# Half loads of the plain block behind runs of seven-product steps, and the second step of the next pair loaded behind the border's plain blocks

## The chip, the cores and the metric

The kernel runs on one core of one Trainium2 chip. The metric is the device time of one execution in microseconds, the median over several runs; lower is better. Matmuls run on TensorE (PE in the profile, its weight loads PEld), element work on VectorE (DVE), ScalarE (ACT) and GpSimd (POOL); SyncE (SP) issues most of the loads.

## What is computed

The reference is one layer of a decoder trunk on 256 tokens (16 meta tokens ahead of them): retention and mLSTM heads with one input and one output projection, and then a gated MLP with a short causal convolution. Only the last part matters here:

```python
up = causal_dwconv(u @ w_up, ffn_conv_w, ffn_conv_b)
gate, val = jnp.split(up, [FFN_DIM], axis=-1)        # FFN_DIM = 5632
h = h + (jax.nn.silu(gate) * val) @ w_down           # (256, 5632) @ (5632, 2048)
return rmsnorm(h, norm_final)[:, N_META:]
```

All is float32.

## The kernel before

**Three products for one.** Every float32 operand is split into a high part (a cast, on ACT) and a low part (operand less high part, on DVE), and a product is made of three matmuls: high by high, low by high, high by low. So for a weight block of 128 x 1024 (`wraw`) ACT writes `whi`, DVE writes `wlo`, and PE takes the block's matmuls with `whi` first and those with `wlo` behind them. `wraw` tiles come from a ring of four, `whi` and `wlo` from rings of five each (`load_w`, L113 to L122). A load into `wraw` waits until the tile that stood in its slot has been read for the last time, by DVE as a rule.

**The down projection.** The FFN is worked on in two halves (L744): 22 tiles of the up projection, and then the down projection over these 22 tiles in 11 *steps* `q` of two tiles (256 rows of `w_down`) each. The 2048 output columns are four blocks `b` of 512, taken in two *pairs* (0, 1) and (2, 3); the 256 tokens are two halves `tt`. Within a pair the steps follow each other in the order of `steps` (L924): 0 to 10, and in the last pair of the second half 0, 1, 4, 2, 7, 3, 5, 6, 8, 9, 10. There are two kinds of steps:

- A *plain* step (`PLAIN`, steps 0, 4, 9, 10; 7 and 8 too in the last pair) loads one block of 512 KB for each `j` of the pair's two column blocks (`load_step`, L909, through L116) and does 12 matmuls of 512 columns with it (`product`, L814, matmuls in L828).
- A *seven-product* step (`FAST`, steps 1, 2, 3, 5, 6, 7, 8) multiplies the 2 x 2 blocks of tokens, rows and columns with seven products in place of eight (`seven`, L830). It loads a sum that was formed early and kept in DRAM (`kept`, 256 KB, L838) and three weight blocks (768 KB, L839) into one of two buffers, `left[turn]`, which take turns (their name in the profile is `hT`, whose memory they use). DVE forms two differences, `ta` (128 x 1024, L842) and the first half of `tb` (128 x 512, L843), in two tiles of the `wraw` ring; the second half of `tb` stays empty. Four casts (L764) and four subtractions (L766) follow, and 21 matmuls (L857, L858, L860).

So steps 1, 2, 3 and 5, 6, 7, 8 stand in runs between the plain steps 0, 4, 9 and 10. At the end of a pair its sums leave PSUM (`share`, L878, and L949) and are added to the result by DMAs of POOL (L876), while the next pair's step 0 begins. That place is called the *border* here.

**What sets the order.** The tile framework orders each engine's instructions by a model of their times; engines then run their rows in order, each waiting for what it needs. `tc.issue_after(x)` forbids an instruction to stand ahead of `x`. A load on SP that must wait for a slot holds up all loads behind it.

Of the kernel before, what the change touches and what calls it, by code (L numbers as in the profile page):

```python
# [11 lines left out]
F32R = mybir.dt.float32r  # L12
# [71 lines left out]
def trunk(ctx: ExitStack, tc: tile.TileContext, io, out: bass.AP):  # L84
# [659 lines left out]
    for half in range(2):  # L744
# [18 lines left out]
        def split(hi, lo, x, after=None):  # L763
            copied = nc.scalar.copy(hi, x)  # L764
            with tc.issue_after(after.ins) if after else nullcontext():
                return copied, nc.vector.tensor_tensor(out=lo, in0=x, in1=hi.bitcast(F32), op=ALU.subtract)  # L766
# [60 lines left out]
            for n, (a, m, i) in list(enumerate(parts))[n0:n1]:  # L827
                nc.tensor.matmul(ps, a, m[:, i, cols], start=first and n == 0, stop=seed or last and n == 5, skip_group_check=seeded)  # L828

        def seven(b, q, cs, ps, first, last, after, norm):  # L830


            nonlocal turn
# [1 line left out]
            raw = left[turn]  # L835
            turn = 1 - turn

            nc.sync.dma_start(raw[:, 0, :], early[b, q])  # L838
            nc.sync.dma_start(raw[:, 1:4, :], io["wd7"][b // 2, half * NQD + q][:, 1:4, :])  # L839
            ta, tb = (wpool.tile([P, 2, 512], F32, name="wraw", bufs=4) for _ in range(2))  # L840

            nc.vector.tensor_tensor(out=ta, in0=raw[:, 0:1, :].to_broadcast([P, 2, 512]), in1=raw[:, 1:3, :], op=ALU.subtract)  # L842
            nc.vector.tensor_tensor(out=tb[:, 0, :], in0=raw[:, 3, :], in1=raw[:, 0, :], op=ALU.subtract)  # L843
# [65 lines left out]
        def load_step(b, q, to=wpool):  # L909
            return load_w(io["wd"][b, half * NQD + q], [P, 2, 512], to)  # L910
# [4 lines left out]
        for b in (0, 2):  # L915
            cs = {}
            for j in range(2):
                for tt in range(2):
                    cs[tt, j] = at.tile([P, 512], F32, name="atps")
            ps = [mm.tile([P, 512], F32, name="mmps") for _ in range(4)]  # L920

            final = half == 1 and b == 2
            steps = [0, 1, 4, 2, 7, 3, 5, 6, 8, 9, 10] if final else range(NQD)
            fast = [q for q in steps if q in FAST and not (final and q in BOTH)]  # L924
            plain = [q for q in steps if q not in fast]
            alone = plain[-lag:] if final else []
            for q in steps:
                if q in fast:
                    due = []
                    if final and q != fast[0]:  # L930
                        due, gains = gains[:1], gains[1:]
                    seven(b, q, cs, ps, q == fast[0], q == fast[-1], emptied, due)
                    if q == fast[-1]:
                        with tc.high_priority() if final else nullcontext():
                            share(ps, b, final)
                    continue
                for j in range(2):
                    if j == 1 and q in alone:
                        continue
                    w = load_step(b + j, q)  # L940
                    for tt in range(2):
                        product(cs[tt, j], tt, q, w, q == plain[0], q == plain[-1 - (lag if final and (tt, j) == (1, 1) else 0)])
            for j in range(2):
                for n, tt in enumerate(range(2)):
                    c = (b + j) * 512
                    if not final:

                        x = x_tile((4, 3, 1, 0)[2 * j + n])
                        emptied = nc.scalar.copy(x, cs[tt, j])  # L949
                        onto(tt, b + j, x)  # L950
                        if half == 1:
                            gains.append((tt, b + j, c, c + 512))
                    elif j == 0:
                        add(cs[tt, j], tt, c)
                        squares(tt, b, c, c + 512)
                        times_gain(tt, c, c + 512)
# [116 lines left out]
```

## Time and profile before

| | us |
|---|---|
| median of three runs | 1205.56 (1204.94 to 1208.27) |
| the profiled execution | 1206.01 |
| its span on the core | 1204.2 |
| down projection, first half of the FFN | 717.5 to 829.2 of the span |
| down projection, second half | 1083.3 to 1196.6 |

The profile is of one execution. Its rows give start and length in us from the start of the span; the time of the whole execution is 1.81 us more than the span. A matmul's row is longer than its share of PE's time, since matmuls overlap: their rate is read from the distance of their starts. Where a row of a timeline ends in brackets, the engine stood idle before it for so long, and the bracket names what ended that.

### The profile page before, as it was taken

The numbers are of one execution on the slowest core, as the hardware profiler recorded it, in microseconds if no ns is written. First come the engines' busy times: TensorE is split into PE (matmuls) and PEld (weight loads), VectorE is DVE, ScalarE is ACT, GpSimd is POOL, SyncE is SP. The second block draws the span as 40 slices with busy tenths as digits, with TensorE's granted clock in tenths as the row PEclk, the third lists the DMA queues.
The fourth block names the chain that finished last, engine by engine and source line by source line (L and its number), as shares of the span: only waits on it lengthen the run. The fifth ranks groups of instructions, "written<-read, shape, count | busy, mean of one in ns | idle before, by whom it ended". The sixth has DMA issues, their size and how long they took to land.

```text
span 1204.2 us, 22798 instructions
## 1 busy us (share of the span) xinstructions
PE 1194.5 (99%) x8956; PEld 1151.2 (96%) x8956; DVE 971.1 (81%) x1446; ACT 708.1 (59%) x964; POOL 167.3 (14%) x222
## 2 busy tenths in 40 slices
PE   9999999999999999999999999999999999999997
PEld 9999999999999999999999998878999999998886
DVE  8967778766775966788888889997697878789897
ACT  8747746655656656555555556665554655556664
POOL 0100001111110311021112100202023112100232
PEclk9999999999999999999999999999999999999999
DMA  8865565566565965766866744949777767755956
GB/s 280 275 208 162 169 187 169 197 182 192 171 189 168 345 204 176 252 219 203 263 217 212 225 178 175 272 182 272 279 249 250 234 247 242 253 184 211 281 170 200
DMA packets 83005, 263.27 MB, mean 219 GB/s; under 512 B 14673, under 2 KB 18897, under 8 KB 82769
## 3 DMA queue, kind: packets, MB, share of 16 engines
q1 hardware_dynamic: 71952, 223.85, 56.9%
q0 software_dynamic: 10368, 37.11, 10.1%
q8 instruction: 70, 1.15, 0.4%
q10 hardware_dynamic: 576, 0.85, 0.2%
q14 instruction: 39, 0.31, 0.1%
HBM read 243.42 MB, written 11.27 MB: 211 GB/s over the span
## 4 chain that ended last, share of the span: by engine, by line
PE 97%; DMA 1%; DVE 1%; ACT 0%; issue 0%; SPq 0%; DVEq 0%; ACTq 0%
PE mmps L128 26%; PE mmps L129 25%; PE mmps L131 25%; PE atps L828 8%; PE mmps L860 2%; PE mmps L857 2%; PE mmps L858 2%; PE atps L858 1%; PE atps L857 1%; PE atps L860 1%; PE atps L380 1%; DMA wraw<-in_wd 1%; PE atps L372 0%; DMA hT<-in_xT 0%; PE atps L128 0%; PE atps L131 0%
## 5 line engine op out<-in xcount | busy, mean ns | idle before, releaser
L119 ACT CAST whi<-wraw 128x1024 fp32r<-128x1024 f32 x352 | 368.5, 1049 | 311.0 <-PE mmps L129 200.9
L121 DVE TENSOR_TENSOR wlo<-wraw,whi 128x1024 fp32r<-128x1024 f32 x352 | 432.5, 1231 | 68.9 <-ACT whi L119 66.7
L128 PE MATMUL mmps<-uh,whi 128*128 128x258 f32 x1408 | 346.1, 283 | 0.0
L129 PE MATMUL mmps<-ul,whi 128*128 128x258 f32 x1408 | 346.0, 283 | 0.0
L128 PEld LDWEIGHTS mmps<-uh,whi 128*128 128x128 f32 x1408 | 267.6, 190 | 0.1
L129 PEld LDWEIGHTS mmps<-ul,whi 128*128 128x128 f32 x1408 | 267.1, 190 | 0.1
L128 PE MATMUL mmps<-xh,whi 128*128 128x272 f32 (+2 forms) x864 | 219.8, 288 | 0.0
L129 PE MATMUL mmps<-xl,whi 128*128 128x272 f32 (+2 forms) x864 | 218.3, 286 | 0.0
L131 PE MATMUL mmps<-uh,wlo 128*128 128x258 f32 x1408 | 196.5, 282 | 0.0
L131 PEld LDWEIGHTS mmps<-uh,wlo 128*128 128x128 f32 x1408 | 179.9, 189 | 0.0
L129 PEld LDWEIGHTS mmps<-xl,whi 128*128 128x128 f32 x864 | 162.9, 189 | 0.0
L128 PEld LDWEIGHTS mmps<-xh,whi 128*128 128x128 f32 x864 | 162.5, 188 | 0.1
L131 PE MATMUL mmps<-xh,wlo 128*128 128x272 f32 (+2 forms) x864 | 126.6, 285 | 0.0
L131 PEld LDWEIGHTS mmps<-xh,wlo 128*128 128x128 f32 x864 | 114.2, 188 | 0.0
L764 ACT CAST whi<-hT 128x1024 fp32r<-128x1024 f32 x52 | 53.6, 1052 | 26.5 <-PE atps L828 7.9
L681 DVE TENSOR_TENSOR cu<-mmps,rstd 128x258 f32<-128x258 f32 x88 | 37.3, 424 | 38.1 <-PE mmps L131 37.5
L766 DVE TENSOR_TENSOR wlo<-hT,whi 128x1024 fp32r<-128x1024 f32 x52 | 62.2, 1221 | 5.9 <-ACT whi L764 4.7
L129 PE MATMUL mmps<-mixl,whi 128*128 128x258 f32 x256 | 63.0, 283 | 0.0
L128 PE MATMUL mmps<-mixh,whi 128*128 128x258 f32 x256 | 62.4, 282 | 0.0
L766 DVE TENSOR_TENSOR wlo<-wraw,whi 128x1024 fp32r<-128x1024 f32 (+1 forms) x52 | 52.2, 1038 | 0.9 <-PE mmps L860 0.2
L764 ACT CAST whi<-wraw 128x1024 fp32r<-128x1024 f32 (+1 forms) x52 | 43.0, 837 | 16.5 <-PE mmps L858 7.1
L876 POOL DMA_DIRECT2D hn<-x x27 | 23.6, 1033 | 202.6 <-ACT x L882 174.8
(284 smaller groups left out, 1732.9 us busy)
## 6 DMA issues: line engine op xcount, KB each, us to landing
wraw<-in_wu SPq DMA_DIRECT2D x176, 512.0 KB, 4.5
wraw<-in_wi SPq DMA_DIRECT2D x108, 512.0 KB, 4.1
hT<-in_wd SPq DMA_DIRECT2D x26, 768.0 KB, 4.6
wraw<-in_wd SPq DMA_DIRECT2D x36, 512.0 KB, 4.9
wraw<-in_wo SPq DMA_DIRECT2D x32, 512.0 KB, 4.1
x<-in_wd POOLq DMA_DIRECT2D x13, 768.0 KB, 7.5
hn<-x POOLq DMA_DIRECT2D x27, 256.0 KB, 7.9
hT<-kept SPq DMA_DIRECT2D x26, 256.0 KB, 2.8
```

The costliest lines, as they stand in the source:

```text
L119: nc.scalar.copy(hi, raw)
L121: nc.vector.tensor_tensor(out=lo, in0=raw, in1=hi.bitcast(F32), op=ALU.subtract)
L128: nc.tensor.matmul(ps, hi[:, k, :], xh(kk), start=kk == first, stop=False)
L129: nc.tensor.matmul(ps, hi[:, k, :], xl(kk), start=False, stop=False)
L131: nc.tensor.matmul(ps, lo[:, k, :], xh(kk), start=False, stop=kk == last)
L681: evacuated = nc.vector.tensor_tensor(out=u, in0=ps[:, :NQ], in1=rstd2, op=ALU.mult)
L764: copied = nc.scalar.copy(hi, x)
L766: return copied, nc.vector.tensor_tensor(out=lo, in0=x, in1=hi.bitcast(F32), op=ALU.subtract)
L828: nc.tensor.matmul(ps, a, m[:, i, cols], start=first and n == 0, stop=seed or last and n == 5, skip_group_check=seeded)
L857: nc.tensor.matmul(o, sh[:, f, m, :], hi[:, i, :], start=begin, stop=False)
L858: nc.tensor.matmul(o, sl[:, f, m, :], hi[:, i, :], start=False, stop=False)
L860: nc.tensor.matmul(o, sh[:, f, m, :], lo[:, i, :], start=False, stop=end)
```

## The change

There are two edits, both in the down projection.

**Half loads.** Where a run of at least two seven-product steps is followed by a plain step, the first block of this plain step (`j` = 0) is no longer loaded into a tile of its own. The second halves of `tb` of the run's last two steps are collected in `spare`, and in the run's last step, behind its own load (`asked`), two loads of 256 KB each fill them. The plain step then casts and subtracts the two halves one after the other (`split`, L764 and L766) into one `whi` and one `wlo`. This happens seven times: at steps 4 and 9 of each pair but the last, and at step 8 of the last pair. The bytes loaded and the matmuls stay the same.

**The held step.** In the second pair of each half (`b == 2`) the load of the second seven-product step may not be issued ahead of the last block load that stands ahead of it in the program (`last_load`, set in `load_w`): that of step 0, `j` = 1, in the first half, and of step 4, `j` = 1, in the second.

```diff
@@ -827,7 +827,7 @@
             for n, (a, m, i) in list(enumerate(parts))[n0:n1]:
                 nc.tensor.matmul(ps, a, m[:, i, cols], start=first and n == 0, stop=seed or last and n == 5, skip_group_check=seeded)
 
-        def seven(b, q, cs, ps, first, last, after, norm):
+        def seven(b, q, cs, ps, first, last, after, norm, held, pieces):
 
 
             nonlocal turn
@@ -835,9 +835,18 @@
             raw = left[turn]
             turn = 1 - turn
 
-            nc.sync.dma_start(raw[:, 0, :], early[b, q])
-            nc.sync.dma_start(raw[:, 1:4, :], io["wd7"][b // 2, half * NQD + q][:, 1:4, :])
+            with tc.issue_after(last_load.ins) if held else nullcontext():
+                nc.sync.dma_start(raw[:, 0, :], early[b, q])
+                asked = nc.sync.dma_start(raw[:, 1:4, :], io["wd7"][b // 2, half * NQD + q][:, 1:4, :])
             ta, tb = (wpool.tile([P, 2, 512], F32, name="wraw", bufs=4) for _ in range(2))
+            for n, i in pieces:
+                if i == 0:
+                    spare.append(tb[:, 1, :])
+                else:
+                    spare.append(tb[:, 1, :])
+                    for i, x in enumerate(spare):
+                        with tc.issue_after(asked.ins):
+                            nc.sync.dma_start(x, io["wd"][b, half * NQD + n][:, i, :])
 
             nc.vector.tensor_tensor(out=ta, in0=raw[:, 0:1, :].to_broadcast([P, 2, 512]), in1=raw[:, 1:3, :], op=ALU.subtract)
             nc.vector.tensor_tensor(out=tb[:, 0, :], in0=raw[:, 3, :], in1=raw[:, 0, :], op=ALU.subtract)
@@ -924,12 +933,15 @@
             fast = [q for q in steps if q in FAST and not (final and q in BOTH)]
             plain = [q for q in steps if q not in fast]
             alone = plain[-lag:] if final else []
-            for q in steps:
+            spare = []
+            for n, q in enumerate(steps):
                 if q in fast:
                     due = []
                     if final and q != fast[0]:
                         due, gains = gains[:1], gains[1:]
-                    seven(b, q, cs, ps, q == fast[0], q == fast[-1], emptied, due)
+                    pieces = [(steps[n + 2 - i], i) for i in range(2)
+                              if steps[n + 2 - i] in plain and all(m in fast for m in steps[n - i : n + 2 - i])]
+                    seven(b, q, cs, ps, q == fast[0], q == fast[-1], emptied, due, b == 2 and q == fast[1], pieces)
                     if q == fast[-1]:
                         with tc.high_priority() if final else nullcontext():
                             share(ps, b, final)
@@ -937,7 +949,13 @@
                 for j in range(2):
                     if j == 1 and q in alone:
                         continue
-                    w = load_step(b + j, q)
+                    if j == 0 and spare:
+                        w = [wpool.tile([P, 2, 512], F32R, name=name, bufs=5) for name in ("whi", "wlo")]
+                        for i, x in enumerate(spare):
+                            split(*(a[:, i, :] for a in w), x)
+                        spare = []
+                    else:
+                        w = load_step(b + j, q)
                     for tt in range(2):
                         product(cs[tt, j], tt, q, w, q == plain[0], q == plain[-1 - (lag if final and (tt, j) == (1, 1) else 0)])
             for j in range(2):
```

In the rows of the changed kernel below, old lines have new numbers: 838 and 839 became 839 and 840, 842 and 843 became 851 and 852, and 857, 858 and 860 became 866, 867 and 869. L849 is the new half load.

On SP, the queue of loads, at the border of the first half and up to step 4 of its second pair. `kept_1` is step 1's early sum, `in_wd` of 128x1536 the rest of the step's load, `wraw<-in_wd` a block of a plain step. Before:

```order
L838 DMA hT<-kept_1_6647 128x512
L839 DMA hT<-in_wd 128x1536
L116 DMA wraw<-in_wd 128x1024 x2
L838 DMA hT<-kept_2_6939 128x512
L839 DMA hT<-in_wd 128x1536
L116 DMA wraw<-in_wd 128x1024 x4
L838 DMA hT<-kept_3_7231 128x512
L839 DMA hT<-in_wd 128x1536
L838 DMA hT<-kept_5_7517 128x512
L839 DMA hT<-in_wd 128x1536
L116 DMA wraw<-in_wd 128x1024 x2
```

After:

```order
L849 DMA wraw<-in_wd 128x512 x2
L839 DMA hT<-kept_1_6647 128x512
L840 DMA hT<-in_wd 128x1536
L116 DMA wraw<-in_wd 128x1024 x5
L839 DMA hT<-kept_2_6939 128x512
L840 DMA hT<-in_wd 128x1536
L839 DMA hT<-kept_3_7231 128x512
L840 DMA hT<-in_wd 128x1536
L849 DMA wraw<-in_wd 128x512 x2
L839 DMA hT<-kept_5_7517 128x512
L840 DMA hT<-in_wd 128x1536
L116 DMA wraw<-in_wd 128x1024
```

Step 2 of the second pair moved from ahead of four block loads to behind them all. Step 9's first block (the first row) now precedes step 1 of the next pair, and step 4's first block precedes step 5's load, where both of its blocks stood behind that before.

On DVE, around step 4 of the same pair: L842 and L843 (L851 and L852) are the differences of steps 5 and 6, L121 and the L766 rows of 128x512 in a pair the subtractions of step 4's blocks. Before:

```order
L842 TENSOR_TENSOR wraw<-hT 128x1024
L121 TENSOR_TENSOR wlo<-wraw,whi 128x1024
L843 TENSOR_TENSOR wraw<-hT 128x512
L121 TENSOR_TENSOR wlo<-wraw,whi 128x1024
L766 TENSOR_TENSOR wlo<-hT,whi 128x1024
L842 TENSOR_TENSOR wraw<-hT 128x1024
L766 TENSOR_TENSOR wlo<-hT,whi 128x1024
```

After:

```order
L851 TENSOR_TENSOR wraw<-hT 128x1024
L766 TENSOR_TENSOR wlo<-wraw,whi 128x512 x2
L121 TENSOR_TENSOR wlo<-wraw,whi 128x1024
L852 TENSOR_TENSOR wraw<-hT 128x512
L851 TENSOR_TENSOR wraw<-hT 128x1024
L766 TENSOR_TENSOR wlo<-hT,whi 128x1024 x2
L852 TENSOR_TENSOR wraw<-hT 128x512
```

The first block's subtraction is two instructions, and step 6's large difference moved ahead of step 5's first subtraction.

On PE at the same place, the end of step 3 (L860, L869: its matmuls with low parts) and the first matmuls of step 4 (L828). Before:

```order
L857 MATMUL atps<-whi,sh 128x512
L858 MATMUL atps<-whi,sl 128x512
L860 MATMUL mmps<-wlo,sh 128x512 x2
L828 MATMUL atps<-whi,mh 128x512
L828 MATMUL atps<-whi,ml 128x512
L828 MATMUL atps<-whi,mh 128x512
L828 MATMUL atps<-whi,ml 128x512
L860 MATMUL mmps<-wlo,sh 128x512 x2
```

After:

```order
L866 MATMUL atps<-whi,sh 128x512
L867 MATMUL atps<-whi,sl 128x512
L828 MATMUL atps<-whi,mh 128x512
L828 MATMUL atps<-whi,ml 128x512
L869 MATMUL mmps<-wlo,sh 128x512 x2
L828 MATMUL atps<-whi,mh 128x512
L828 MATMUL atps<-whi,ml 128x512
L869 MATMUL mmps<-wlo,sh 128x512 x2
```

The first two matmuls of step 4 stand ahead of two of step 3's matmuls that they followed before.

## The prediction

> **What bounds the kernel now.** I read the page's busy shares first, then the two stages that the change touches.
>
> ```profile
> PE 1194.5 (99%) x8956; PEld 1151.2 (96%) x8956; DVE 971.1 (81%) x1446; ACT 708.1 (59%) x964; POOL 167.3 (14%) x222
> ```
>
> TensorE is busy for 1194.5 of 1204.2 us. A busy PE could still be waiting inside its matmuls, so I looked at the view by stretches: the down projection of the first half of the FFN, then that of the second (columns: length, then busy time and count of PE, PEld, DVE, ACT, POOL).
>
> ```profile
> 717.50:829.20 111.70, 110.92 (x484) 90.42 (x484) 100.90 (x106) 68.64 (x78) 10.54 (x12) 1.00 0.67 215
> 1083.30:1196.60 113.30, 113.30 (x518) 93.39 (x516) 102.81 (x114) 71.74 (x93) 24.33 (x22) 1.00 0.67 215
> ```
>
> In the first stretch 484 matmuls take 111.70 us, 0.231 each. The clock column is 1.00. What one costs with nothing in its way stands in the chain of waits, whose rows around the first of two stalls are (start, length, what):
>
> ```profile
> 786.95 1.15 DVE wlo L766
> 788.11 3.62 DMA wraw<-in_wd
> 791.83 1.06 ACT whi L119
> 792.93 1.21 PE atps L828 x4
> ...
> 794.82 3.66 PE atps L828 x16
> ...
> 813.75 3.41 DMA wraw<-in_wd
> 817.26 1.06 ACT whi L119
> ```
>
> Sixteen matmuls in 3.66 us are 0.229 each, and 484 of those are 110.8 us: the stage is at the matmuls' own rate but for about 0.9 us. The chain seems to say more, since from 786.95 to 792.93 it runs through DVE, a load and a cast; but a chain shows what the last wait hung on, not how long PE stood. That is in the list of PE's waits (line, releaser, us in total, times, longest), which for the whole kernel is three rows:
>
> ```profile
> PE atps L199 <- DVE ones L169: 1.1, 1, 1.1
> PE atps L828 <- ACT whi L119: 0.8, 2, 0.4
> PE atps L128 <- ACT whi L226: 0.3, 1, 0.3
> ```
>
> Only the middle row is in the change's reach. PE's own timeline gives its full size:
>
> ```profile
> 791.94 0.62 PE L860 MATMUL mmps<-wlo,sh 128*128 128x512 f32 x2
> 792.93 0.51 PE L828 MATMUL atps<-whi,mh 128*128 128x512 f32 x1 [0.36 <-ACT whi L119]
> 793.27 0.40 PE L828 MATMUL atps<-whi,ml 128*128 128x512 f32 x1
> ...
> 817.32 0.63 PE L860 MATMUL mmps<-wlo,sh 128*128 128x512 f32 x2
> 818.36 0.50 PE L828 MATMUL atps<-whi,mh 128*128 128x512 f32 x1 [0.42 <-ACT whi L119]
> 818.70 0.40 PE L828 MATMUL atps<-whi,ml 128*128 128x512 f32 x1
> ...
> 1176.03 0.50 PE L828 MATMUL atps<-whi,sh 128*128 128x512 f32 x1
> 1176.36 0.40 PE L828 MATMUL atps<-whi,sl 128*128 128x512 f32 x1
> ```
>
> By starts: two matmuls from 791.94 leave room for the next at 792.40; it came at 792.93 (0.53 late), and its successor 0.34 later where 0.23 is the rule (0.11). Together 0.64 us. In the same way 0.58 + 0.11 = 0.69 at 818.36, and 0.10 at 1176.03. **All that the change can win is 0.64 + 0.69 + 0.10 = 1.43 us.**
>
> **The change part by part.** *The earlier load.* All three places are the first plain block behind a run of seven-product steps: step 4 and step 9 of the second pair in the first half, step 8 at the end. Before, its load waited for a slot of the ring of four that the run's own differences fill: 788.11 is where the subtraction of 786.95 ends, and from there load, cast and matmul follow without a gap. After, the block goes into the free halves of the last two steps' smaller tiles; the load is asked right behind that of the last step.
>
> ```profile
> 777.71 0.33 SPq L838 DMA_DIRECT2D hT<-kept  x1
> 778.09 1.03 SPq L839 DMA_DIRECT2D hT<-in_wd  x1
> ...
> 805.13 0.59 SPq L839 DMA_DIRECT2D hT<-in_wd  x1
> ```
> ```profile
> 777.60 1.82 DVE L766 TENSOR_TENSOR wlo<-wraw,whi 128x1024 fp32r<-128x1024 f32 x2
> 785.12 1.23 DVE L842 TENSOR_TENSOR wraw<-hT 128x1024 f32<-128x1024 f32 x1 [2.67 <-DMA hT<-in_wd]
> ```
> ```profile
> 787.01 1.79 ACT L764 CAST whi<-wraw 128x1024 fp32r<-128x1024 f32 x2
> 813.81 0.62 ACT L764 CAST whi<-wraw 128x512 fp32r<-128x512 f32 x1 [0.66 <-DVE wlo L766]
> ```
>
> At step 4 the last step's load leaves SP by 779.1. The second piece also waits for its tile's former user, step 1, whose last subtractions end at 779.4. So both pieces are under way by 780.3, behind a load that has landed by 785.1; half a megabyte at the stretch's 215 GB/s is 2.4 us more: **about 787.5**, against 791.7 before. ACT is busy with step 3 until 788.8 and then casts two pieces of 0.62 us: ready by 790.1, and PE asks at 791.94. At step 9 the pieces go out at 805.7 and 806.1; even with the slowest row for a load of 512 KB below, 7.6, they are there by 813.7, ACT is free at 814.4, ready by 815.7, and PE asks at 817.3. Both stalls go, with some 1.7 us to spare, and the smaller third likewise. Next in line is the block's other half, which now waits for the slot that the first half waited for before (788.11): it lands at 791.8 and is wanted only after the eight matmuls of the first half and five left over from step 3, 791.94 + 13 x 0.229 = 794.9.
>
> *More instructions.* Seven blocks are loaded, cast and subtracted in two pieces: 7 more loads on SP, 7 casts on ACT, 7 subtractions on DVE.
>
> ```profile
> L121 DVE TENSOR_TENSOR wlo<-wraw,whi 128x1024 fp32r<-128x1024 f32 x16 | 19.3, 1223 | 3.8 <-ACT whi L119 3.6 <-PE mmps L860 0.2
> L766 DVE TENSOR_TENSOR wlo<-wraw,whi 128x512 fp32r<-128x512 f32 x14 | 9.6, 686 | 0.1
> ```
>
> Two small subtractions cost 2 x 686 - 1223 = 149 ns more, 1.0 us in seven places. DVE is busy 101 of 111.7 us here, so none of it is on the path as long as PE's backlog hides it; without that cover the price is 0.15 us at a place. I take nothing; bounds 0 and +1.0. By the Trainium skill, "Perfetto Trace Analysis", section "Optimizing Scalar/DVE Operations", a DVE instruction on SBUF carries about 60 ns of access overhead, and grouping pays if the engine is saturated; that would be an estimated 7 x 60 = 420 ns. The row's 149 ns holds more than that, since the profiled time counts an end that overlaps the next instruction; the sum stays the same by either.
>
> The two pieces also hold their tiles until they are subtracted, so the later loads of a border wait for them: from the order of DVE that is one or two subtractions of 0.69 us later for block 10. Its wait is covered by plain blocks, which PE works on for 24 x 0.229 = 5.5 us a step.
>
> *The held step.* At the change of pair the load of the second seven-product step leaves its place ahead of four block loads and goes behind them.
>
> ```profile
> 758.71 0.33 SPq L838 DMA_DIRECT2D hT<-kept  x1
> ...
> 759.85 4.02 SPq L116 DMA_DIRECT2D wraw<-in_wd  x4
> ```
> ```profile
> wraw<-in_wd SPq DMA_DIRECT2D x1, 512.0 KB, 7.6
> hT<-in_wd SPq DMA_DIRECT2D x1, 768.0 KB, 6.9
> ```
> ```profile
> 773.48 1.22 DVE L842 TENSOR_TENSOR wraw<-hT 128x1024 f32<-128x1024 f32 x1
> ```
>
> The first row of a landing is the last of those four, issued at 763.5: there at 771.1. The second is step 3's, at 778.09. The same megabytes in another order end at the same time, so the held step lands at about 771 to 772 (issued at about 764.2, and with 6.9: 771.5). DVE needs it at 773.48: **no cost, 1.5 us of room.** The four blocks, one megabyte lighter ahead of them, come earlier. In the second half there are six:
>
> ```profile
> 1139.38 0.33 SPq L116 DMA_DIRECT2D wraw<-in_wd  x1
> ```
> ```profile
> 1153.83 1.07 PE L828 MATMUL atps<-wlo,mh 128*128 128x512 f32 x4
> ```
>
> The last block's load went at 1139.38; the held step follows by 1140.2 and lands by 1147.8 (7.6). Behind it DVE has two differences and the block's own subtraction, 1.23 + 0.69 + 1.23 = 3.2 us: 1151.0, and PE takes that result at 1153.83.
>
> **The sum.** The profiled execution took 1206.01 us, of which the span is 1204.2. Less 1.43: 1204.6. The median of the three runs is 0.45 lower, so for a median I forecast 1205.56 - 1.43 = 1204.13, say **1204.1 us**, 0.12% less. A measurement of this kernel can tell about 0.3% (3.6 us) from no change, so this counts as the same.
>
> **The rivals.**
>
> *The stalls only move.* DVE is the engine behind PE's feed: a seven-product step gives it four operations of about 1.22 us and two of 0.69, 6.3 us (ends overlap a little), and PE 21 x 0.229 = 4.8. If PE then waits for a subtraction instead of a cast, or a piece's load is late, 0 to 1.43 us come back, and the seven splits add up to 1.0: between 1204.1 and 1206.6, likeliest 1205.5. Against it: the list has no wait of PE for DVE in either stage.
>
> *Slower: the held load is late.* Of all that is queued on DVE behind step 2's difference, step 1's subtractions are the tight ones: they free the buffer for step 3's load (777.71), and step 3's data are what DVE waits 2.67 us for at 785.12. PE takes the first cast of it here:
>
> ```profile
> 787.59 0.39 PE L857 MATMUL atps<-whi,sh 128*128 128x512 f32 x1
> ```
>
> The cast is done at about 786.1, so 1.5 us are free; a held load that lands after 773.5 + 1.5 = 775.0 costs PE a microsecond for each that it is late. With the slowest landing behind a fully queued border, 764.2 + 12.3 (the time from 758.71 to 771.1) = 776.5, that is 1.5 us; twice that for both halves, with the win kept, 1205.7, and 1207.1 without. For 0.3% it must be 5 us over both halves.
>
> *The change does not do what it says*, because SP does not get to the pieces sooner: 1205.6. The program order says it does.
>
> *Larger pieces were better.* By the Trainium skill, "Perfetto Trace Analysis", section "DMA Optimizations", larger loads use HBM better, which speaks against halves; the same list has it that splitting lets some work start sooner. As a mechanism of this kernel it is the queue: a shorter load lands hardly sooner.
>
> ```profile
> hT<-kept SPq DMA_DIRECT2D x12, 256.0 KB, 2.8
> wraw<-in_wd SPq DMA_DIRECT2D x14, 512.0 KB, 4.4
> ```
>
> Two of 2.8 us in turn are 5.6 against 4.4, 1.2 us later at each place; the 1.7 us to spare cover it, so 1204.1 stands.
>
> **How the numbers follow.** Forecast 0.62; stalls move or nothing happens 0.22; late held load, within 0.3%, 0.06; beyond 0.3%, 0.06 with whatever else slows it; the larger pieces' price, beyond its cover, 0.02; an unforeseen gain 0.02. The gain is capped by the rows at 1.4 us, so faster by over 0.3% has 0.02, slower 0.06, the same 0.92. The range takes the rivals up to 1207.1 and the spread of the three runs (-0.6 and +2.7 about their median): **1202.8 to 1207.6**.
>
> **What would show it.** Right: PE's waits lose the row of L828, the first plain block's load stands on SP straight behind the last step's and lands at least a microsecond before its cast, and the first stretch shrinks by 1.3 us. Wrong in the step of the pieces: PE waits for L766 casts or subtractions at the first plain block. Wrong in the held step: DVE idles at the differences of the second pair's step 2 for its load, and step 3 starts late on PE.

## The result and the profile after

The changed kernel takes **1216.77 us** (median of 6 runs, 1215.14 to 1218.42), the kernel before in the same job 1207.66 (6 runs, 1204.94 to 1208.91). The ratio is 1.0081, with a 95% interval of 1.0068 to 1.0095: **slower by 9.1 us**, where 1.4 less was forecast. The profiled execution took 1216.82 us, its span 1215.0, so 10.8 us more than the span before. The other numbers of the profile come from this execution.

The busy shares of the page hardly differ, as they count a PE that runs on without saying what it does:

```profile
PE 1198.0 (99%) x8956; PEld 1150.5 (95%) x8956; DVE 968.1 (80%) x1453; ACT 707.2 (58%) x971; POOL 171.8 (14%) x222
```

Where the 10.8 us lie is read from PE's timeline of the changed kernel: the first matmul of the down projection and the first of its last group (four matmuls in the first half, two in the second), first half and second (start, length, what).

```profile
718.55 0.39 PE L828 MATMUL atps<-whi,mh 128*128 128x512 f32 x1
...
832.95 0.39 PE L828 MATMUL atps<-wlo,mh 128*128 128x512 f32 x1
...
1086.29 0.39 PE L828 MATMUL atps<-whi,mh 128*128 128x512 f32 x1
...
1206.90 0.28 PE L828 MATMUL atps<-wlo,mh 128*128 128x256 f32 x1
```

From start to start the first half takes 832.95 - 718.55 = 114.40 us and the second 1206.90 - 1086.29 = 120.61. In the kernel before, the same four rows start at 717.55, 829.84, 1083.33 and 1196.21: 112.29 and 112.88. So **2.1 us are lost in the first half and 7.7 in the second**. The stage begins 1.0 us later, from the wait at L128 below, far ahead of the down projection; what lies between the halves and behind them is the same to 0.2.

The list of PE's waits (line, releaser, us in total, times, longest) had one row in reach of the change. Now it has five, those of L828 and L869:

```profile
PE atps L828 <- DVE wlo L121: 2.6, 3, 1.4
PE mmps L869 <- DVE wlo L766: 2.1, 4, 0.7
PE atps L828 <- ACT whi L119: 1.3, 1, 1.3
PE atps L128 <- ACT whi L226: 1.1, 1, 1.1
PE atps L199 <- DVE ones L169: 1.1, 1, 1.1
PE atps L869 <- DVE wlo L766: 0.7, 1, 0.7
PE atps L828 <- ACT x L967: 0.3, 1, 0.3
```

PE now waits 5.4 us (2.6 + 2.1 + 0.7) for subtractions of DVE, for which it did not wait once before. (The rows undercount: by the distances of the starts each wait costs some 0.3 us more than its row.) Most of it is in the second half, and DVE's timeline shows why (in brackets: idle before, and what ended it):

```profile
1148.74 1.22 DVE L121 TENSOR_TENSOR wlo<-wraw,whi 128x1024 fp32r<-128x1024 f32 x1
1155.88 1.23 DVE L851 TENSOR_TENSOR wraw<-hT 128x1024 f32<-128x1024 f32 x1 [5.92 <-DMA hT<-in_wd]
```

**DVE, the engine that feeds PE, stands idle for 5.92 us, and what ends it is the held step's load.** SP's queue at that place:

```profile
1123.89 18.87 SPq L116 DMA_DIRECT2D wraw<-in_wd  x7
1142.86 1.74 SPq L839 DMA_DIRECT2D hT<-kept  x1
1144.65 1.28 SPq L840 DMA_DIRECT2D hT<-in_wd  x1
1147.12 0.33 SPq L839 DMA_DIRECT2D hT<-kept  x1
```

Seven block loads go out one by one as ring slots come free, until 1142.8, and only then does the held step's load leave. Before, it went ahead of them, on a span in which the second half began 3.0 us earlier:

```profile
1124.05 0.43 SPq L839 DMA_DIRECT2D hT<-in_wd  x1
```

Issue itself takes 1.74 and 1.28 us, where about 0.3 and 0.4 are common. The DMA view of the changed kernel from 1144 to 1148 (queue: packets, MB, share of the engines' time; then what was issued, KB, us to landing):

```profile
q0 software_dynamic: 299, 0.55, 77.2%
q1 hardware_dynamic: 137, 0.50, 30.8%
issues: line engine op xcount, KB each, median us to landing
hT<-in_wd SPq DMA_DIRECT2D x2, 768.0 KB, 11.1
```

The accumulations of POOL's queue, with which the first pair's results are added, take 77% of the engines' time just then, and the held load lands after 11.1 us: 1144.65 + 11.1 = 1155.8. That the accumulations make it so late was not tested: before, a load of the same kind that was issued at 1143.79, with these at 105.6% from 1144 to 1148 by the same view, landed after 7.9 us.

PE's timeline shows what the late load costs. These are its waits from there to 1190:

```profile
1158.90 1.19 PE L828 MATMUL atps<-wlo,mh 128*128 128x512 f32 x4 [1.42 <-DVE wlo L121]
1165.15 0.51 PE L869 MATMUL atps<-wlo,sh 128*128 128x512 f32 x1 [0.70 <-DVE wlo L766]
1172.00 0.73 PE L869 MATMUL mmps<-wlo,sh 128*128 128x512 f32 x2 [0.38 <-DVE wlo L766]
1180.07 0.72 PE L869 MATMUL mmps<-wlo,sh 128*128 128x512 f32 x2 [0.73 <-DVE wlo L766]
1185.17 0.74 PE L869 MATMUL mmps<-wlo,sh 128*128 128x512 f32 x2 [0.48 <-DVE wlo L766]
```

By the distances of the starts PE lost nothing from 1086.29 to 1156, then 5.7 us up to 1186: 2.0 at the block that comes right behind the held differences, and 3.7 in the four waits after it, since DVE did not make up for its idle time. The last 1.9 us were lost at the final plain steps (1196 to 1201), where half loads alone lose 1.7.

In the first half PE stood 3.3 us by the distances of its starts, where it stood 1.3 before. Half of that, 1.6 us, is at the end. The chain of waits there:

```profile
820.90 0.69 DVE wlo L766
821.59 0.02 issue
821.61 6.57 DMA wraw<-in_wd
828.18 0.02 issue
828.20 0.02 ACTq L119
828.22 0.04 issue
828.26 1.05 ACT whi L119
829.31 0.04 issue
829.35 0.74 PE atps L828 x2
```

Block 10's second load waits for a subtraction of step 9's halves (820.90), as these sit in the tile whose slot it needs; load and cast follow without a gap, and PE stands for 1.33 us (of the 1.3 of L828 <- ACT whi).

### The profile page after: what moved, and what is told of

Its sections match the earlier page's. It is cut to its first block, busy times and chain, and to the rows that moved or that the text cites. A ratio compares the mean times of both kernels' runs of the same rounds, so it can differ in the third digit from the quotient of the medians.

```text
span 1215.0 us, 22834 instructions
## 1 busy us (share of the span) xinstructions
PE 1198.0 (99%) x8956; PEld 1150.5 (95%) x8956; DVE 968.1 (80%) x1453; ACT 707.2 (58%) x971; POOL 171.8 (14%) x222
## 4 chain that ended last, share of the span: by engine, by line
PE 94%; DMA 3%; DVE 2%; issue 1%; ACT 0%; SPq 0%; DVEq 0%; ACTq 0%
PE mmps L128 25%; PE mmps L129 25%; PE mmps L131 25%; PE atps L828 5%; PE mmps L866 2%; PE mmps L867 2%; PE mmps L869 2%; DMA wraw<-in_wd 1%; PE atps L869 1%; PE atps L867 1%; PE atps L866 1%; DVE wlo L766 1%; DMA hn<-x 1%; PE atps L380 1%; PE atps L372 0%
## 5 line engine op out<-in xcount | busy, mean ns | idle before, releaser
L119 ACT CAST whi<-wraw 128x1024 fp32r<-128x1024 f32 x345 | 360.4, 1048 | 270.1 <-PE mmps L129 164.5
L121 DVE TENSOR_TENSOR wlo<-wraw,whi 128x1024 fp32r<-128x1024 f32 x345 | 424.6, 1232 | 69.2 <-ACT whi L119 68.3
L128 PE MATMUL mmps<-uh,whi 128*128 128x258 f32 x1408 | 346.1, 283 | 0.0
L128 PEld LDWEIGHTS mmps<-uh,whi 128*128 128x128 f32 x1408 | 267.6, 190 | 0.1
L128 PE MATMUL mmps<-xh,whi 128*128 128x272 f32 (+2 forms) x864 | 219.9, 288 | 0.0
L128 PEld LDWEIGHTS mmps<-xh,whi 128*128 128x128 f32 x864 | 162.6, 188 | 0.1
L764 ACT CAST whi<-hT 128x1024 fp32r<-128x1024 f32 x52 | 53.5, 1050 | 30.6 <-DMA hT<-in_wd 12.9
L766 DVE TENSOR_TENSOR wlo<-hT,whi 128x1024 fp32r<-128x1024 f32 x52 | 61.9, 1218 | 5.9 <-ACT whi L764 5.2
L128 PE MATMUL mmps<-mixh,whi 128*128 128x258 f32 x256 | 62.4, 282 | 0.0
L764 ACT CAST whi<-wraw 128x1024 fp32r<-128x1024 f32 (+1 forms) x66 | 50.5, 789 | 18.3 <-PE mmps L867 4.8
L766 DVE TENSOR_TENSOR wlo<-wraw,whi 128x1024 fp32r<-128x1024 f32 (+1 forms) x66 | 57.6, 911 | 0.8 <-PE atps L869 0.4
```

Of the source, the lines that this page charges most:

```text
L119: nc.scalar.copy(hi, raw)
L121: nc.vector.tensor_tensor(out=lo, in0=raw, in1=hi.bitcast(F32), op=ALU.subtract)
L128: nc.tensor.matmul(ps, hi[:, k, :], xh(kk), start=kk == first, stop=False)
```

## The experiments

Each kernel ran in five rounds beside the kernel before, in the same job, and its time is the median. The table gives the ratio with its interval, and the length of the two down projections in the profiled execution, read as above.

| run | us | ratio to before | first half | second half |
|---|---|---|---|---|
| before | | 1 | 112.3 | 112.9 |
| the change | 1216.77 | 1.0081 (1.0068 to 1.0095) | 114.4 | 120.6 |
| half loads alone | 1210.05 | 1.0019 (1.0008 to 1.0030) | 114.6 | 115.5 |
| hold alone | 1211.53 | 1.0031 (1.0020 to 1.0041) | 113.8 | 117.6 |
| half loads, hold in the first half | 1209.83 | 1.0021 (1.0012 to 1.0030) | 114.8 | 115.5 |
| half loads, hold in the second half | 1216.80 | 1.0071 (1.0059 to 1.0083) | 115.7 | 120.0 |
| the change, held behind step 0 | 1212.82 | 1.0051 (1.0033 to 1.0069) | 114.0 | 116.0 |
| half loads at step 4 alone | 1209.30 | 1.0022 (1.0011 to 1.0034) | 112.6 | 113.9 |
| half loads at steps 9 and 8 alone | 1211.38 | 1.0037 (1.0024 to 1.0050) | 113.5 | 116.4 |
| half loads, own tile in the second half | 1208.70 | 1.0015 (1.0004 to 1.0027) | 112.8 | 112.6 |
| the same, no half loads in the first half | 1207.30 | 0.9997 (0.9987 to 1.0007) | 112.4 | 112.6 |
| own tile, hold in the second half | 1217.74 | 1.0084 (1.0070 to 1.0098) | 115.9 | 121.5 |
| own tile, held behind step 0 | 1215.59 | 1.0069 (1.0056 to 1.0081) | 117.0 | 119.3 |
| the change, sums together | 1214.73 | 1.0058 (1.0044 to 1.0072) | 113.4 | 118.8 |
| own tile, behind step 0, sums together | 1210.99 | 1.0027 (1.0016 to 1.0039) | 117.8 | 116.2 |
| own tile, hold in second half, sums together | 1211.02 | 1.0030 (1.0019 to 1.0041) | 114.4 | 114.8 |

The lengths are of one execution each, and executions differ: the first half has the same source in five rows (half loads, no hold in that half) and reads 112.8 to 115.9 there, so a single reading of it is good to some 2 us. The second half repeats better: 115.5 twice with half loads and no hold there, 112.6 twice with the tile of its own, 120.0 and 120.6 with half loads and the hold. A profiled execution can also lie off its kernel's median: that of before, 1206.01, is 1.5 under the 1207.53 of the second job, that of half loads alone, 1211.05, is 1.0 over, that of step 4 alone, 1207.16, is 2.1 under, and that of "own tile, behind step 0, sums together", 1215.77, is 4.8 over. So a length compared with before can overstate a loss by 2.5 us in all for half loads alone, and by 6.3 in the worst row.

### The parts of the change

Half loads alone:

```diff
-                    seven(b, q, cs, ps, q == fast[0], q == fast[-1], emptied, due, b == 2 and q == fast[1], pieces)
+                    seven(b, q, cs, ps, q == fast[0], q == fast[-1], emptied, due, False, pieces)
```

> Half loads without the held step (the second step's load keeps its old place ahead of the border's blocks). Theory H (the held load of the second half lands late, DVE stands 5.9 us, PE pays about 7.4 us later): those 7.4 us go, the stall of 1.5 us at the end of the first half stays; about 1208 to 1210 where before gives 1207.7. Theory P (the split blocks are the cause: more instructions, tiles held longer): stays at 1215 to 1217. Theory B (only both together cost): 1206 to 1208.

The hold alone:

```diff
-                    pieces = [(steps[n + 2 - i], i) for i in range(2)
-                              if steps[n + 2 - i] in plain and all(m in fast for m in steps[n - i : n + 2 - i])]
+                    pieces = []
```

> The held step without half loads. Theory H: 1213 to 1216, with DVE standing 4 us or more at the large difference of step 2 in the last pair, for its load. Theory P: 1207 to 1208, as before. Theory B: 1206 to 1208.

Half loads with the hold in one half only, the first or the second:

```diff
-                    seven(b, q, cs, ps, q == fast[0], q == fast[-1], emptied, due, b == 2 and q == fast[1], pieces)
+                    seven(b, q, cs, ps, q == fast[0], q == fast[-1], emptied, due, half == 0 and b == 2 and q == fast[1], pieces)
```

(and `half == 1` in the other)

> Half loads as changed, the held step in the first half of the FFN alone. Theory H, and the cost sits in the second half: 1208 to 1211, no stall of PE above 0.3 us in the last pair. If the cost of holding were the same in both halves: 1211 to 1214. Theory P: 1215 to 1217.

> Half loads as changed, the held step in the second half alone. Theory H: 1214 to 1217, the first half's share of the held step being below 1.5 us. Theory P: 1215 to 1217.

Measured: half loads +2.5 us beside the kernel before in their job (1207.53), with the hold of the first half no more (+2.3), with that of the second +9.3, the whole change again. So **the first half's hold costs nothing that these runs can see, the second half's about 7 us beside half loads, the hold of both halves alone 4, and half loads about 2.5**. Theory H had half loads at 1208 to 1210, which 1210.05 just misses, and the hold alone at 1213 to 1216, where 1211.53 came. It also allowed PE no stall above 0.3 us in the last pair with the hold in the first half, where there were two, of 0.66 and 0.55, and half loads alone have 0.67 there. In the profiles the hold's part of the second half is steadier: 117.6 - 112.9 = 4.7 alone, 120.0 - 115.5 = 4.5 and 120.6 - 115.5 = 5.1 beside half loads. DVE's idle time ahead of the held differences was 4.95 us with the hold alone and 5.60 with half loads and the hold of the second half.

With the hold alone, SP's row of the held load, its landing, and DVE's row of the held difference are these:

```profile
1140.19 0.43 SPq L840 DMA_DIRECT2D hT<-in_wd  x1
```
```profile
hT<-in_wd SPq DMA_DIRECT2D x1, 768.0 KB, 11.3
```
```profile
1151.63 1.22 DVE L851 TENSOR_TENSOR wraw<-hT 128x1024 f32<-128x1024 f32 x1 [4.95 <-DMA hT<-in_wd]
```

The load leaves when the prediction had it leave (1140.2), and without a long issue; measured from the start of the second half, 1085.18 here, it leaves even 1.9 us sooner. It still takes 11.3 us. So the late issue of the changed kernel is not needed for DVE's wait; the slow landing is enough.

### The held load earlier

```diff
-            with tc.issue_after(last_load.ins) if held else nullcontext():
+            with tc.issue_after(held.ins) if held else nullcontext():
...
-                    seven(b, q, cs, ps, q == fast[0], q == fast[-1], emptied, due, b == 2 and q == fast[1], pieces)
+                    seven(b, q, cs, ps, q == fast[0], q == fast[-1], emptied, due, mark if b == 2 and q == fast[1] else None, pieces)
...
+                if q == plain[0]:
+                    mark = last_load
```

> The changed kernel with one edit: in both halves the held load goes behind the loads of step 0, so that in the second half it stands behind five of the seven block loads at the border, and the two of step 4 follow it (in the first half nothing moves). Theory H (the held load of the second half simply comes too late, 5.9 us idle on DVE at its differences): they find their data without a wait, the wait of 5.92 us at line 851 around 1150 is under 1.5 us, and the time falls to that of the half loads with a hold in the first half alone, 1209.8, at most 1211.5. Theory C (the queue is full there whatever the order, because the block accumulations of GpSimd's queue run beside it): the wait moves to step 4's blocks and the time stays at 1214 to 1217.

SP's queue of this kernel, and then from its DVE timeline the held differences:

```profile
1124.03 7.28 SPq L116 DMA_DIRECT2D wraw<-in_wd  x5
1131.36 0.42 SPq L839 DMA_DIRECT2D hT<-kept  x1
1131.83 1.35 SPq L840 DMA_DIRECT2D hT<-in_wd  x1
1140.80 2.06 SPq L116 DMA_DIRECT2D wraw<-in_wd  x2
```
```profile
1148.19 1.82 DVE L766 TENSOR_TENSOR wlo<-wraw,whi 128x1024 fp32r<-128x1024 f32 x2
1149.93 1.22 DVE L851 TENSOR_TENSOR wraw<-hT 128x1024 f32<-128x1024 f32 x1
```

Two places earlier in the queue is 12.8 us earlier in time, 1131.83 for 1144.65 (1.0 of it since the whole second half began 1.0 us earlier). The wait of 5.92 us is gone, and the second half is at 116.0, half a microsecond over half loads without any hold. That is theory H and not C. The median came to 1212.8 and not under 1211.5, so the time bears out a good half of what was expected: 4 of 7 us. The load took 11.1 us to land here too; it only had the time.

### What the half loads cost

At step 4 alone, or at steps 9 and 8 alone, without a hold:

```diff
-                              if steps[n + 2 - i] in plain and all(m in fast for m in steps[n - i : n + 2 - i])]
+                              if steps[n + 2 - i] == 4 and all(m in fast for m in steps[n - i : n + 2 - i])]
```

(and `in plain[-3:]` for the other)

> No hold; half loads at step 4 alone (three places: three of the seven), step 9 and step 8 loaded whole as before. Theory T (the half loads cost where they keep a tile of the ring from the next blocks at the end of a pair): nothing is lost, the stall of 0.64 us at step 4 goes, so 1206.5 to 1207.7 beside 1207.5 for the kernel before. Theory P (every split costs, some 0.33 us a place of 2.3 in seven): 1208.5, and below that of the four other places.

> No hold; half loads at step 9 (three places) and step 8 of the last pair alone, step 4 loaded whole. Theory T: all of the half loads' 2.3 us is here and the won stall of step 4 is not, so 1210 to 1210.8. Theory P (every split costs alike): 1207.5 + 4/7 x 2.5 = 1209.0 or less.

Neither theory had either number: step 4 alone cost 2.4 us (its 12 runs went from 1206.2 to 1213.5), the ends 4.4, more than all seven together. The lengths point to theory T, with 0.3 and 1.0 us lost at step 4 and 1.2 and 3.5 at the ends, but do not settle it, as the profiled execution of step 4 alone was one of its fastest. So the suspected cost was taken away: in the second half, where memory is free, the halves got a tile of their own.

```diff
-                if i == 0:
-                    spare.append(tb[:, 1, :])
-                else:
-                    spare.append(tb[:, 1, :])
+                if half == 0:
+                    spare.append(tb[:, 1, :])
+                elif i == 1:
+                    own = more.tile([P, 2, 512], F32, name="own", bufs=1)
+                    spare.extend(own[:, k, :] for k in range(2))
+                if i == 1:
```

> No hold; half loads at all seven places; in the second half (where memory is free) the two pieces go into a tile of their own instead of the free halves of the ring's tiles, in the first half as in the change. Profiles so far, from the first to the last matmul of the down projection: second half 112.9 us before, 115.5 with half loads alone. Theory T (the tiles held keep the next blocks' loads back): the second half is back at 112.7 to 113.6, the time about 2 us under that of half loads alone, some 1208 where the kernel before has 1207.3. Theory P (the extra instructions and short loads themselves cost): the second half stays at 115 or above.

The second of the two also has no half loads in the first half (`half == 1 and` ahead of the condition):

> As the run before, and no half loads in the first half, so nothing of the change is left but three places of half loads in a tile of their own. Theory T: both halves as in the kernel before (112.3 and 112.7 to 113.6 us), the time within 0.1% of it. Theory P: the second half 115 or above, the time 2 us over the kernel before.

Theory T, in both: the second half is at 112.64 us in each, against 115.5 with the halves in the ring's tiles, with the same extra loads, casts and subtractions. **In the second half the half loads themselves cost nothing; what cost there, by the profiles, was that the ring's tiles stayed occupied.** With the halves in the ring's tiles, the chain of waits at the end of that half runs, as in the first, from a subtraction on L766 through a block's load (5.96 us from 1181.64) to DVE and PE. The medians say less: from half loads alone to the tile of its own the loss beside before goes from 2.5 to 1.45 us, which the intervals do not tell apart. The second run is level with the kernel before (0.9997). It is no gain either: in this half there was 0.10 us to win.

### Two runs that missed

With the tile of its own, the hold of the second half was put back, late as in the change, and early:

> The kernel with half loads and a tile of their own in the second half, with the hold of the second half added as the change has it. Theory H (the hold stands by itself: the held megabyte waits on SP's queue behind blocks that wait for ring slots): the second half grows from 112.6 us by the 4.8 of the hold alone (117.6 in that run against 112.9 before) to 117 to 118, the time to about 1213; at its differences DVE waits 5 us. Theory B (much of the loss is only made by held tiles and hold together): 113 to 115, time 1209 to 1210.

> The change with both its costs taken out as far as they can be: a tile of their own for the half loads of the second half, and in the second half the held load behind step 0's blocks (five or six) instead of step 4's. Theories H and T: no wait of DVE over 1.5 us at the held differences, second half 112.6 to 113.6 us, first half as in the other runs with half loads, 112.8 to 114.8; time 1207.5 to 1209.5, level with the kernel before within 0.2% and not under it. Rival: any hold in the second half costs, second half 115 or above, time over 1210.5.

In the first both theories fell: it came to 121.5 us in the second half. In the second the rival's numbers came (119.3 us, 1215.59), though not by way of DVE. In neither did DVE wait for the held load; ACT and then PE waited for something else. ACT's timeline of the late one:

```profile
1139.89 0.59 ACT L969 COPY x<-atps 128x512 f32<-128x512 f32 x1 [0.38 <-PE atps L828]
1142.31 0.59 ACT L969 COPY x<-atps 128x512 f32<-128x512 f32 x1 [1.83 <-DMA hn<-x]
1152.02 0.59 ACT L969 COPY x<-atps 128x512 f32<-128x512 f32 x1 [9.12 <-DMA hn<-x]
```

This is the copy of the first pair's results out of PSUM (L949 before). It waits 9.12 us until an `x` tile has been accumulated (`hn<-x`), and PE cannot begin the next pair in that bank. The tile is late as the sums that fill it are late (`share`): on DVE they stand scattered among block subtractions that themselves wait for loads.

```profile
1134.23 0.69 DVE L895 TENSOR_TENSOR x<-mmps,x 128x512 f32<-128x512 f32 x1
...
1140.80 0.68 DVE L898 TENSOR_TENSOR x<-x,mmps 128x512 f32<-128x512 f32 x1
1141.40 0.68 DVE L904 TENSOR_TENSOR x<-x,mmps 128x512 f32<-128x512 f32 x1
```

Nothing in the edits asks for that; the framework orders DVE anew when loads move. In the kernel before the four stand together:

```profile
1128.43 0.68 DVE L884 TENSOR_TENSOR x<-mmps,x 128x512 f32<-128x512 f32 x1
1129.21 0.69 DVE L885 TENSOR_TENSOR x<-mmps,x 128x512 f32<-128x512 f32 x1
1130.00 0.69 DVE L887 TENSOR_TENSOR x<-x,mmps 128x512 f32<-128x512 f32 x1
1130.61 0.68 DVE L893 TENSOR_TENSOR x<-x,mmps 128x512 f32<-128x512 f32 x1
```

In the changed kernel they are scattered too, the first at 1131.97 and the last ending at 1138.86 + 0.68 = 1139.5. So the last three runs hold the second half's block subtractions behind the four sums, in the changed kernel and in the two that missed:

```diff
+        with tc.issue_after(summed.ins) if summed else nullcontext():
-        nc.vector.tensor_tensor(out=lo, in0=raw, in1=hi.bitcast(F32), op=ALU.subtract)
+            nc.vector.tensor_tensor(out=lo, in0=raw, in1=hi.bitcast(F32), op=ALU.subtract)
...
-            nc.vector.tensor_tensor(out=x5, in0=x7, in1=p5, op=ALU.subtract)
+            done = nc.vector.tensor_tensor(out=x5, in0=x7, in1=p5, op=ALU.subtract)
+            if half == 1 and b == 0:
+                summed = done
```

> The changed kernel, with one thing fixed on DVE's queue: in the second half the four sums of the first pair's shared products stay together, ahead of the next blocks' subtractions, as they stood in the kernel before; the scheduler had put them between those subtractions, and they ended at 1139.5 instead of 1131.3. Theory H (the held load itself is late): the wait of some 5 us at the held differences stays, the second half is still 118.5 to 120.6 us, the time within 2 us of the change's 1216.8. Theory S (the sums, by way of the accumulations that follow them, delay the loads and copies, and the hold only shifts them): the wait falls under 2 us and the second half to 114 to 116.

> The kernel with a tile of its own for half loads in the second half and the held load behind step 0's blocks, now with the four sums together as before. Theory S+H+T (three costs: late held load, tiles held, sums scattered; all three out): ACT's copies of the first pair's results no longer wait 9 us for an accumulation, PE's wait of 3.4 us for them goes, the second half is 112.6 to 114 us, and the time 1208 to 1211 with the first half's 2 us left. Rival N (the hold in the second half costs in any form): the second half stays at 116 or above.

> The kernel with a tile of its own for half loads in the second half and the hold as the change has it, now with the four sums together. Theory S+H: of 121.5 us in the second half the wait of 5.9 us for the copies goes and the hold's own 4.8 comes up: 116.5 to 118, the time about 1212. If the hold's loss was all by way of the sums: 113 to 114, the time 1208 to 1210.

The two that missed gain 4.6 and 6.7 us (1215.59 to 1210.99, 1217.74 to 1211.02), so the scattered sums were the most of their loss. The early one's time is in the range of "all three out", but its second half, at 116.2, is the rival's (in an execution 4.8 us over the median); the late one's, at 114.8, came between its two cases. Both are still 3.2 us over the kernel before, where the tile of its own without a hold was 1.45 over. So a hold in this half cost something in every form tried, though here the intervals overlap. The changed kernel gains only 2.0 (1216.77 to 1214.73): the second half falls to 118.8 as theory H had it, but the wait at the held differences goes too, as theory S had it. The wait has moved: PE stands 2.27 us at 1142.68, again for that copy, which now stands on ACT behind the cast of a block for whose load ACT was idle 5.67 us; and PE's next matmuls run at half rate (last section). The held load is no earlier for it: it goes at 1144.29 and lands after 9.1 us, at 1153.4, and DVE finds it there because DVE itself gets to it only at 1153.53. So putting the sums together is worth some 2 us, but the runs do not show that their order makes the load late, as each repair of the order moves something else.

## Why the prediction was wrong

- **What bounds the kernel, and the cap on the gain: right.** PE without slack, and 1.43 us to win. Such a kernel has little to win and all its cover to lose.
- **The earlier load: right, but no gain.** The halves are cast in time, and the stalls of 792.93 and 818.36 are gone. PE stands elsewhere instead, in the first half 0.49 us for a subtraction of a step and 1.33 us for block 10. This is the rival "the stalls only move", with DVE as the engine it named.
- **More instructions: right at nothing.** Half loads with a tile of their own left the second half at 112.64 us and the time at 0.9997 of before.
- **The two pieces hold their tiles: wrong, the smaller step that failed.** I put it at "one or two subtractions of 0.69 us later for block 10" and covered by plain blocks. The subtraction is that late, but its load comes with it and took 6.57 us to land, at the end of a stage where the blocks that should cover it wait in the same ring. All half loads together measured 2.5 us in the time. In the second half's profile they measured 2.6 (115.5 against 112.9), all of which went when the tile was not held; in the first half, where that wasn't tried, the cause rests on the chain of waits alone.
- **The held step, first half: right.** No cost that shows in the two runs that tell it apart (1209.83 with, 1210.05 without).
- **The held step, second half: wrong, and most of the loss.** The step that failed reads: "The last block's load went at 1139.38; the held step follows by 1140.2 and lands by 1147.8 (7.6)." The landing was mis-sized: 11.3 us with the hold alone, where the load did leave at 1140.19, and 11.1 in the changed kernel. There it left at 1144.65, of which 3.0 us are only that the whole second half began later (1086.29 for 1083.33); measured from that start, it left 1.5 us and landed 5.0 us later than forecast. I had taken 7.6 from the border of the first half.
- **What a late load costs, second half: wrong too.** Before, DVE ran the held difference here:

```profile
1145.04 1.22 DVE L842 TENSOR_TENSOR wraw<-hT 128x1024 f32<-128x1024 f32 x1
```

So even a landing at 1147.8 made DVE wait. I counted that as free, since I compared the block's subtraction with one matmul, that of 1153.83, which left 2.8 us of room. At that matmul the changed kernel lost 2.0 us, and the hold alone almost nothing (0.2). But DVE is busy 102.8 of 113.3 us in this stage, and what it stood idle (5.92 and 4.95 us) was paid in the following steps: 3.7 us more in the changed kernel, 3.6 with the hold alone.

- **Not in the prediction at all:** that the framework would order DVE anew, with the first pair's sums among block subtractions. It stands in the order of the changed kernel, which at the border I read on SP alone.
- **The rival "the held load is late" was the mechanism that came**, and its size was off. It was priced in the first half, where there was room, and given 0.06 beyond 0.3%, since I doubled the first half's 1.5 us rather than work the second half out. Even that sum is wrong: twice 1.5 us on 1204.1 is 1207.1 with the win kept and 1208.6 without it, not 1205.7 and 1207.1.

What stays open is why the held load took 11 us to land (POOL's accumulations and the loads queued beside it are the candidates), and whether the scattered sums have a part in that.

## What to carry to other kernels

A load queue that waits in order for ring slots turns any load put behind it into one that waits for them all: here two blocks' difference in place was some 12 us in time. A late input is not paid at its first use alone: where the engine that it stops has little slack, the idle time comes back over the steps that follow. A free half of a tile is not free if the tile's ring is what the next loads wait for; price it by the landing of the load that is put back. And where a scheduler orders the engines, read its order for the engine that feeds the bottleneck, and not only for the queue that was edited.

## What the runs showed of the hardware

After some of its waits of 2 us and more, PE ran at half rate. The late hold with a tile of its own has the longest, 5.94 us for the copy shown above; the view by stretches of that kernel, ahead of the wait, right behind it, and later (the last columns are the granted clock, DMA share, GB/s):

```profile
1143.00:1146.00 3.00, 3.00 (x15) 2.47 (x14) 0.00 (x0) 0.00 (x0) 2.35 (x3) 1.00 1.05 279
1152.70:1157.50 4.80, 4.80 (x12) 3.80 (x13) 3.92 (x4) 4.38 (x6) 1.47 (x2) 0.52 0.74 130
1158.00:1162.00 4.00, 4.00 (x19) 3.27 (x18) 4.00 (x5) 3.37 (x4) 0.00 (x0) 1.00 0.94 334
```

Twelve matmuls took 4.80 us where nineteen take 4.00: a granted clock of 0.52, and 4.80 - 12 x 0.229 = 2.05 us lost on top of the wait. The same came behind waits of 2.04, 2.15, 2.27 and 3.44 us in other runs (a clock of 0.50 to 0.54 over the next 3 us), but not behind one of 2.55. The Trainium skill, "TensorE: Matmul & The Clock Gate", section "Part 1: The HAM clock gate (the "warmup" mystery)", has the array at half rate after an idle window of about 3.4 us that runs freely of the kernel. A window that runs freely would agree with a longer wait that goes unpunished, but 2.04 us is too short to hold one of 3.4 us. In the changed kernel's own profile no wait of the down projection reached 1.5 us, so this is no part of its loss.
